# Layer-1 modulation vectors as spread half sums with their own load and sum tiles, in a two-layer hybrid trunk

## Chip, cores and metric

The kernel runs on one core of one Trainium2 chip. The metric is device microseconds of one execution, the median of three runs. Engines are named as the profile has them: TensorE (PE, with its weight load PEld), VectorE (DVE), ScalarE (ACT), GpSimd (POOL) and SyncE (SP). SP and POOL issue the DMAs here. Every engine takes its instructions in order.

## What is computed

A trunk of two layers over 1,024 tokens of width 1,024, in float32. Each layer has a mixer (attention in layer 0; retention beside an S5 state-space model in layer 1) and a convolutional feed-forward net. Both are preceded by an RMS norm that is scaled and shifted, and followed by a gate; shift, scale and gate come from the condition `c` by one large matrix per layer:

```python
cond = jax.nn.silu(c)
for i in range(DEPTH):
    mod = cond @ mod_w[i] + mod_b[i]
    sh1, sc1, g1, sh2, sc2, g2 = jnp.split(mod, 6, axis=-1)
    h = modulated_rmsnorm(x, norm1_g[i], sh1, sc1)
    ...
    x = x + g1[:, None, :] * mixed
    h = modulated_rmsnorm(x, norm2_g[i], sh2, sc2)
    x = x + g2[:, None, :] * conv_ffn(h, ffn_w_in[i], ffn_conv_w[i], ffn_conv_b[i], ffn_w_out[i])
return rmsnorm(x, final_g).astype(x.dtype)
```

`mod_w` is 2 x 1024 x 6144. The six vectors are numbered j = 0 to 5 (sh1, sc1, g1, sh2, sc2, g2), each in two halves of 512.

## The kernel before

Matrix products are made three times, with the operands split into a high and a low part (`mm3`, lines 134 to 136). Weights come by SP into a tile `stage` of 128 x 1024 (two buffers), ScalarE rounds it to the high part `wH` (line 124), VectorE subtracts to get the low part `wL` (line 125). Work that is ready is ordered by a scheduler in the tile framework: by the order of the code, with weights moved ahead by `high_priority`, and with instructions put earlier where their engine would stand idle in the scheduler's reckoning. What a reader finds in the code is therefore not the order on an engine.

The program runs in stages: start and first mixer (to about 540 us), output projection and first up phase (`up7`, PSUM tiles `c`, to about 1,080), first down phase (`down22`, tiles `acc`, to about 1,365) with the S5 constants beside it, second mixer (`mixer1`, from `mixer1_head`, to about 1,740), its output projection (`out_proj`, tiles `lin`), second up phase (to about 2,260), second down phase, final norm.

One **half sum** (`mod_sum`, lines 521 to 533) is half a vector of `cond @ mod_w`: eight loads of 128 x 512 by SP (256 KB each, line 528) into the ring `pn`, eight products on VectorE (the first at line 530, seven at line 532) into a tile of the ring `ma`, then in `mod_cols` (line 539) four matmuls with a column of ones (line 545) that add over the partitions, and a small VectorE addition of the bias (line 548). For j = 1 and 4 `mod_scale` makes the norm's scale from it. `pn` has four buffers and `ma` two, and both are general rings: the up phase's intermediate `s1`, the projections, S5 constants and the GLU's sigmoid (line 1376) take tiles of `pn` too.

Seven half sums of layer 0 are made in the first mixer, between heads. The other 13 come by `mod_all`: (layer 0, j 5, second half) at step 0 of the first down phase; layer 1's j 0 and 1 at steps 6 and 15 of it; j 2, 3 and 4 as steps M2, M3 and M4 of the retention order `RET_STEPS`; j 5 at step 2 of the second down phase. In `RET_STEPS` R0 to R3 are the heads in three parts, P projections, V values, H the load of S5 results, G the GLU (four parts). A head's last part stores its rows by POOL to DRAM (`mixd`), and the output projection loads them again (`mix`).

Of the kernel before, what the change touches and what calls it, by code (L numbers as in the profile page):

```python
# [10 lines left out]
F32 = mybir.dt.float32  # L11
# [3 lines left out]
ALU = mybir.AluOpType  # L15
# [5 lines left out]
KD = D // 128  # L21
# [8 lines left out]
S5_STEPS = 'S0 S1 X S2 P0 V0 S3 P0 V1'  # L30
RET_STEPS = 'R0 V2 P1 R0 R1 R0 R1 P1 V3 R2 R1 M2 H G R2 M3 R2 G R3 M4 G R3 R3 G'
EPS = 1e-6
# [63 lines left out]
class Trunk:  # L96
# [437 lines left out]

    def mod_all(self, l, j, ps, tag, halves=(0, 1), **kw):
        for half in halves:
            self.mod_cols(l, j, half, self.mod_sum(l, j, half), ps, tag, **kw)

# [550 lines left out]
    def mixer1(self):  # L1089
        nc, i = self.nc, self.i  # L1090
        w = i["od_w_in"][0]
        with self.pool("qkv", bufs=1) as qp, self.pool("m1ps", bufs=2, space=PSUM) as ps:
# [26 lines left out]
            def step(what):  # L1119
                kind, n = what[0], int(what[1:] or 0)  # L1120
                if kind in "RPG":
                    if what not in todo:
                        todo[what] = self.retain(n, pairs, V, rp, ps) if kind == "R" else \
                            self.project1(w, n, pairs, rp if n else qp, ps) if kind == "P" else self.glu(ps)
                    next(todo[what], None)
                else:
                    {"V": lambda: v(n), "S": lambda: s5(n), "X": gate3, "H": load_y, "M": lambda: self.mod_all(1, n, ps, "ta", bufs=3)}[kind]()

            with self.pool("wx1", bufs=2) as wx, self.pool("s5", bufs=1) as sp:
                self.wpools = [self.wp, wx]  # L1130
                for what in S5_STEPS.split():
                    step(what)
                self.wpools = [self.wp]
            with self.pool("ret", bufs=1) as rp:
                for what in RET_STEPS.split():
                    step(what)
            self.load_mix(0, 0, 4)

# [247 lines left out]
    def out_proj(self, w, l, xT, hf, x, ps, group=1, order=range(KD), between=None, fetch=False, ahead=AHEAD):  # L1386

        nc = self.nc
        hs = slice(hf * 512, hf * 512 + 512)
        for n0 in range(0, KD, group):  # L1390
            if between and n0 in TILES:
                next(between, None)
            ns = range(n0, n0 + group)
            Ws = [self.weights(w, 0, n * 128, ahead=AHEAD if n0 else ahead) for n in ns]
            if fetch:
                with self.tc.issue_after(self.loaded):
                    for n in ns:
                        nc.sync.dma_start(xT[:, n, hs], self.xs[:, n, hs])
                    if hf == 0 and n0 in (2, 4):
                        self.load_mix(1, n0 - 2, n0 + 2, 2, nc.sync)  # L1400
            for n, p in zip(ns, self.products(Ws, x, hf, ps, order=order)):
                nc.vector.scalar_tensor_tensor(xT[:, n, hs], p, self.mod[l][:, 16 + n:17 + n], xT[:, n, hs],
                                               ALU.mult, ALU.add)
# [49 lines left out]
    def up7(self, l, blocks, free, wxs, Gd):  # L1453
# [10 lines left out]
        with self.pool(f"u7ps{l}", bufs=1, space=PSUM) as ps:  # L1464
# [111 lines left out]

            Q = [{} for _ in range(NF + 2)]
            next(prep)
            for ft in range(PRE):
# [13 lines left out]
            with self.pool(f"late{l}", bufs=1) as late:  # L1593
# [6 lines left out]
                for ft in range(NF):  # L1600
                    q, n, m = Q[ft], Q[ft + 1], Q[ft + 2]
                    p6(ft, q)
                    if ft + 2 < NF:
                        head(ft + 2, m, ft + 2 < PRE)
                        if ft + 2 >= PRE:
                            p1(ft + 2, m)
                    p7(ft, q)
                    if ft + 1 < NF:
                        third(ft + 1, n)
# [72 lines left out]
    def run(self, stages=("mix0", "ffn0", "mix1", "ffn1")):  # L1682
        nc = self.nc
        with self.pool("cst", bufs=1) as self.cst, self.pool("dr", bufs=1, space=DRAM) as self.dr, \
                self.pool("wp", bufs=2) as self.wp, self.pool("tp", bufs=1) as self.tp, \
                self.pool("hp", bufs=1) as self.hp:
            self.wpools = [self.wp]
            self.s5c = self.dr.tile([4, 128, 4096], F32, name="s5c")
            with self.pool("lin", bufs=2, space=PSUM) as self.lin:
                self.mixer0(self.begin())  # L1690
            G0 = self.first_ffn_up()
            with self.pool("ub", bufs=1) as ub:
                with self.pool("s5p", bufs=1) as self.s5p, self.pool("xp", bufs=1) as xp, \
# [4 lines left out]
                    def apart(what):  # L1698
# [5 lines left out]
                        return hook  # L1704
                    hooks = {0: [lambda ps, tag: self.mod_all(0, 5, ps, tag, (1,))], 26: [apart(self.s5_small)]}
                    for j in range(2):
                        hooks[6 + 9 * j] = [lambda ps, tag, j=j: self.mod_all(1, j, ps, tag)]
                    for b in range(4):
# [7 lines left out]
                    self.mixer1_head(xT, ub, ps)  # L1716
                    self.wpools = [self.wp]
                self.mixer1()
            self.last_layer()

    def ffn_up(self, l, project):

        with contextlib.ExitStack() as es:
# [6 lines left out]
            with self.pool(f"opps{l}", bufs=4, space=PSUM) as ps:  # L1730
                w4 = X0.rearrange("p a b n -> p (a b n)").rearrange("p (a n) -> p a n", n=1024)
                self.wpools = [self.wp, Slots(wH=[w4[:, 0], w4[:, 1]], wL=[w4[:, 2], w4[:, 3]])]
                xT = project(xp, ps)
                self.wpools = [self.wp]
                self.store_x(xT, 1)
# [11 lines left out]
    def last_layer(self):  # L1747
# [10 lines left out]
        with self.pool("xp3", bufs=1) as xp, self.pool("fin", bufs=1) as fin, self.pool("wb", bufs=2) as wb, \  # L1758
# [5 lines left out]
            with self.pool("dnps", bufs=2, space=PSUM) as ps:  # L1764
                self.down22(1, xT, Gd, wb, wc, ps, lambda ps, tag: self.finish(xT, 0, ps, tag),
                            {2: [lambda ps, tag: self.mod_all(1, 5, ps, tag)]}, (self.wp, wb, wc))
            with self.pool("finps", bufs=4, space=PSUM) as ps:
# [39 lines left out]
```

## Time and profile before

| | |
|---|---|
| median of three runs | 2550.88 us (2543.54 to 2551.49) |
| profiled execution, its own time | 2545.7 us |
| its span | 2544.0 us |
| busy: PE, PEld, DVE, ACT, POOL | 95%, 78%, 72%, 45%, 7% |
| DMA | 391.56 MB, mean 154 GB/s |
| loads of modulation weights after the start | 160, 256 KB each |

A busy share is a mean over stages with different limits. PE counts as busy from the start of a matmul to its modelled end, so a full PE can still be slowed; the granted clock tells that apart. What a place costs is read from that place: how long PE stands there, at which clock, and what it waited for.

### The profile page before, as it was taken

The numbers are of one execution on the slowest core, as the hardware profiler recorded it, in microseconds if no ns is written. First come the engines' busy times: TensorE is split into PE (matmuls) and PEld (weight loads), VectorE is DVE, ScalarE is ACT, GpSimd is POOL, SyncE is SP. The second block draws the span as 40 slices with busy tenths as digits, with TensorE's granted clock in tenths as the row PEclk, the third lists the DMA queues.
The fourth block names the chain that finished last, engine by engine and source line by source line (L and its number), as shares of the span: only waits on it lengthen the run. The fifth ranks groups of instructions, "written<-read, shape, count | busy, mean of one in ns | idle before, by whom it ended". The sixth has DMA issues, their size and how long they took to land.

```text
span 2544.0 us, 32732 instructions
## 1 busy us (share of the span) xinstructions
PE 2421.3 (95%) x11599; PEld 1992.1 (78%) x11599; DVE 1839.5 (72%) x3383; ACT 1144.1 (45%) x1764; POOL 190.7 (7%) x356
## 2 busy tenths in 40 slices
PE   6999999999899999989989999979989999989997
PEld 5788888888688888877777777867868888878886
DVE  6777776666887877868996545575798787775554
ACT  4556566674544444334443344323454443424442
POOL 1000000032000000000000211201000000000000
PEclk7999999999999999999999999879999999999999
DMA  8455444466132222388774542567422222258562
GB/s 303 127 143 145 141 137 144 141 227 223 60 103 80 86 84 80 126 294 279 230 235 143 169 133 94 183 198 252 146 75 88 79 87 84 79 184 279 182 224 91
DMA packets 323524, 391.56 MB, mean 154 GB/s; under 512 B 28641, under 2 KB 203350, under 8 KB 322848
## 3 DMA queue, kind: packets, MB, share of 16 engines
q1 hardware_dynamic: 294848, 293.45, 37.3%
q0 software_dynamic: 28512, 96.02, 10.5%
q8 instruction: 91, 1.49, 0.2%
q14 instruction: 73, 0.60, 0.1%
HBM read 292.73 MB, written 70.30 MB: 143 GB/s over the span
## 4 chain that ended last, share of the span: by engine, by line
PE 71%; DVE 11%; DMA 8%; ACT 4%; issue 4%; SPq 1%; POOL 0%; DVEq 0%; ACTq 0%; POOLq 0%
PE c L136 10%; PE c L135 10%; PE c L134 10%; PE acc L135 6%; PE acc L136 6%; PE lin L134 5%; PE lin L135 5%; PE acc L134 5%; PE lin L136 5%; DMA pn<-in_mod_w_dram 2%; DVE wL L125 2%; DMA mix<-mixd 1%; DVE ma L532 1%; PE ta L738 1%; PE S L715 1%
## 5 line engine op out<-in xcount | busy, mean ns | idle before, releaser
L124 ACT ACTIVATE wH<-stage 128x1024 fp32r<-128x1024 f32 x372 | 393.0, 1059 | 538.0 <-PE acc L136 154.9
L125 DVE TENSOR_TENSOR wL<-stage,wH 128x1024 fp32r<-128x1024 f32 x372 | 452.9, 1220 | 207.3 <-ACT wH L124 200.8
L135 PE MATMUL acc<-wL,wH 128*128 128x512 f32 x704 | 280.2, 398 | 11.7 <-DVE wL L125 11.6
L136 PE MATMUL acc<-wH,wL 128*128 128x512 f32 x704 | 278.7, 396 | 0.0
L134 PE MATMUL acc<-wH 128*128 128x512 f32 x704 | 275.5, 397 | 3.2 <-DVE t2k L1568 2.4
L134 PE MATMUL lin<-h,wH 128*128 128x512 f32 x576 | 233.5, 405 | 6.2 <-ACT h L422 5.4
L135 PE MATMUL lin<-h,wH 128*128 128x512 f32 x576 | 233.7, 406 | 0.0
L136 PE MATMUL lin<-h,wL 128*128 128x512 f32 x576 | 230.3, 400 | 0.0
L134 PE MATMUL c<-h,wH 128*128 128x512 f32 x528 | 208.4, 395 | 9.2 <-ACT t2k L1589 6.5
L135 PE MATMUL c<-X,wH 128*128 128x512 f32 x528 | 207.2, 392 | 5.9 <-DVE X L1439 5.9
L134 PE MATMUL c<-X,wH 128*128 128x512 f32 x528 | 207.4, 393 | 2.6 <-ACT X L1438 2.4
L136 PE MATMUL c<-h,wL 128*128 128x512 f32 x528 | 207.0, 392 | 0.9 <-DVE wL L125 0.9
L136 PE MATMUL c<-X,wL 128*128 128x512 f32 x528 | 206.6, 392 | 0.0
L135 PE MATMUL c<-h,wH 128*128 128x512 f32 x528 | 206.4, 391 | 0.0
L135 PEld LDWEIGHTS acc<-wL,wH 128*128 128x128 f32 x704 | 134.9, 192 | 43.3 <-DVE wL L125 15.7
L134 PEld LDWEIGHTS acc<-wH 128*128 128x128 f32 x704 | 134.3, 191 | 32.5 <-DVE t2k L1568 3.2
L136 PEld LDWEIGHTS acc<-wH,wL 128*128 128x128 f32 x704 | 134.6, 191 | 28.1
L134 PEld LDWEIGHTS lin<-h,wH 128*128 128x128 f32 x576 | 110.2, 191 | 27.1 <-ACT h L422 5.7
L134 PEld LDWEIGHTS c<-h,wH 128*128 128x128 f32 x528 | 99.6, 189 | 35.8 <-ACT t2k L1589 7.3
L135 PEld LDWEIGHTS lin<-h,wH 128*128 128x128 f32 x576 | 110.2, 191 | 20.6 <-DVE h L425 1.4
L136 PEld LDWEIGHTS lin<-h,wL 128*128 128x128 f32 x576 | 110.2, 191 | 20.1 <-issue 0.2
L135 PEld LDWEIGHTS c<-X,wH 128*128 128x128 f32 x528 | 99.8, 189 | 27.5 <-DVE X L1439 6.7
(498 smaller groups left out, 5020.1 us busy)
## 6 DMA issues: line engine op xcount, KB each, us to landing
stage<-in_ffn_w_in_dram SPq DMA_DIRECT2D x92, 512.0 KB, 4.0
stage<-in_ffn_w_out_dram SPq DMA_DIRECT2D x176, 256.0 KB, 3.7
stage<-Gd SPq DMA_DIRECT2D x176, 256.0 KB, 4.0
pn<-in_mod_w_dram SPq DMA_DIRECT2D x160, 256.0 KB, 3.3
Gd<-ca POOLq DMA_DIRECT2D x88, 256.0 KB, 2.6
mix<-mixd POOLq DMA_DIRECT2D x52, 256.0 KB, 5.8
stage<-in_ev_w_in_dram SPq DMA_DIRECT2D x24, 512.0 KB, 4.0
xT<-xs SPq DMA_DIRECT2D x48, 256.0 KB, 5.1
```

The source lines that it names most:

```text
L124: nc.scalar.activation(wh[:, :n], st[:, :n], AF.Copy)
L125: nc.vector.tensor_tensor(wl[:, :n], st[:, :n], f(wh[:, :n]), ALU.subtract)
L134: nc.tensor.matmul(ps, wh, xh, start=s, stop=False)
L135: nc.tensor.matmul(ps, wh, xl, start=False, stop=False)
L136: nc.tensor.matmul(ps, wl, xh, start=False, stop=e)
L532: nc.vector.scalar_tensor_tensor(acc, st, self.cond[:, t:t + 1], acc, ALU.mult, ALU.add)
L715: nc.tensor.matmul(dst, q, KH[:, kk], start=True, stop=False)
L738: nc.tensor.transpose(pt[:, kk, j * 128:j * 128 + 128], W[j][:, (a + kk) * 128:(a + kk) * 128 + 128], self.ident)
```

## The change

The 13 late half sums are made by a generator, `mod_slow`: each step issues the next load and one product, and the ones-matmuls of a finished half sum follow at the third step of the next one. `mod_on` advances it by so many steps. The loads have tiles of their own (`ms`, two buffers), the sums too (`md`, two), in a new pool `dp`; its 8 KB per partition come from the space of POOL's software descriptors, halved to 8192 bytes. Calls stand in each tile of both up phases, at steps 2 to 25 of the first down phase, after each step of the second mixer, and six in each group of the output projection's first half. `mod_all` and the steps M2, M3 and M4 are gone.

```diff
-RET_STEPS = 'R0 V2 P1 R0 R1 R0 R1 P1 V3 R2 R1 M2 H G R2 M3 R2 G R3 M4 G R3 R3 G'
+RET_STEPS = 'R0 V2 P1 R0 R1 R0 R1 P1 V3 R2 R1 H G R2 R2 G R3 G R3 R3 G'
...
-    def mod_all(self, l, j, ps, tag, halves=(0, 1), **kw):
-        for half in halves:
-            self.mod_cols(l, j, half, self.mod_sum(l, j, half), ps, tag, **kw)
+    def mod_slow(self, todo):
...
+        def load(l, j, half, t):
+            st = self.dp.tile([128, 512], F32, tag="ms", name="ms", bufs=2)
+            c0 = j * 1024 + half * 512
+            nc.sync.dma_start(st, self.i["mod_w"][l, t * 128:t * 128 + 128, c0:c0 + 512])
+            return st
+        steps = [(*c, t) for c in todo for t in range(KD)]
+        left, st = [], load(*steps[0])
+        where = yield
+        for n, (l, j, half, t) in enumerate(steps):
+            x, st = st, load(*steps[n + 1]) if n + 1 < len(steps) else None
+            if t == 0:
+                acc = self.dp.tile([128, 512], F32, tag="md", name="md", bufs=2)
+                nc.vector.tensor_scalar(acc, x, self.cond[:, 0:1], None, ALU.mult)
+            else:
+                nc.vector.scalar_tensor_tensor(acc, x, self.cond[:, t:t + 1], acc, ALU.mult, ALU.add)
+            if t == KD - 1:
+                left.append((l, j, half, acc))
+            elif t == 2 and left:
+                c = left.pop()
+                self.mod_cols(*c, *where[:2], **where[2])
+            where = yield
+        yield
+        c = left.pop()
+        self.mod_cols(*c, *where[:2], **where[2])
...
                 for what in S5_STEPS.split():
                     step(what)
+                    self.mod_on(1, ps, "ta", bufs=3)
...
                 for what in RET_STEPS.split():
                     step(what)
+                    self.mod_on(1, ps, "ta", bufs=3)
...
+            if l and not hf:
+                self.mod_on(6, ps, "lin")
             for n, p in zip(ns, self.products(Ws, x, hf, ps, order=order)):
...
+            slow = lambda: self.mod_on(1, Banks(bank), "x")
...
                     p7(ft, q)
+                    slow()
...
+            self.mod_begin([(0, 5, 1)] + [(1, j, half) for j in range(2) for half in range(2)])
             G0 = self.first_ffn_up()
...
-                    hooks = {0: [lambda ps, tag: self.mod_all(0, 5, ps, tag, (1,))], 26: [apart(self.s5_small)]}
-                    for j in range(2):
-                        hooks[6 + 9 * j] = [lambda ps, tag, j=j: self.mod_all(1, j, ps, tag)]
+                    hooks = {s: [lambda ps, tag: self.mod_on(1, ps, tag)] for s in range(2, 26)}
+                    hooks[26] = [apart(self.s5_small)]
...
+                self.mod_begin([(1, j, half) for j in (2, 3, 4) for half in range(2)])
                 self.mixer1()
...
+                if l:
+                    self.mod_begin([(1, 5, half) for half in range(2)])
...
-                            {2: [lambda ps, tag: self.mod_all(1, 5, ps, tag)]}, (self.wp, wb, wc))
+                            {}, (self.wp, wb, wc))
...
-    nc = bacc.Bacc("TRN2", target_bir_lowering=False, num_devices=1)
+    nc = bacc.Bacc("TRN2", target_bir_lowering=False, num_devices=1, dynamic_dma_scratch_size=8192)
```

Three places show how instructions move. On SP in the first mixer, where the copies of the second head's keys (KH, KL) go out, before:

```order
L183 DMA KH<-pn 64x512
L183 DMA KL<-pn 64x512
L183 DMA KH<-pn 64x512 x4
L183 DMA KL<-pn 64x512 x4
L110 DMA stage<-in_ev_w_in_dram 128x8x128
L528 DMA pn<-in_mod_w_dram 128x512 x8
```

and in the change:

```order
L183 DMA KH<-pn 64x512
L183 DMA KL<-pn 64x512
L542 DMA ms<-in_mod_w_dram 128x512 x4
L183 DMA KH<-pn 64x512 x2
L183 DMA KL<-pn 64x512 x2
L183 DMA KH<-pn 64x512
L183 DMA KL<-pn 64x512
L183 DMA KH<-pn 64x512
L183 DMA KL<-pn 64x512
L110 DMA stage<-in_ev_w_in_dram 128x8x128
L542 DMA ms<-in_mod_w_dram 128x512 x5
L528 DMA pn<-in_mod_w_dram 128x512 x4
```

Nine loads of late half sums (`ms`) now stand between the key copies and ahead of the loads of layer 0's own sums (`pn`).

On VectorE in the second mixer, the last retention head (R3): `o` is its output, `rs` the Newton steps of its norm. Before:

```order
L1259 TENSOR_TENSOR o<-ta,T 128x256
L1259 TENSOR_TENSOR o<-ta,T 128x512
L1261 TENSOR_TENSOR o<-o,av 128x256
L1261 TENSOR_TENSOR o<-o,av 128x512
L1265 TENSOR_TENSOR o<-o,g 128x1024
L562 TENSOR_SCALAR rs<-ta 128x8
L218 TENSOR_SCALAR rs<-rs 128x8
```

and in the change:

```order
L1298 TENSOR_TENSOR o<-ta,T 128x256
L553 SCALAR_TENSOR_TENSOR md<-ms,small,md 128x512
L1300 TENSOR_TENSOR o<-o,av 128x256
L553 SCALAR_TENSOR_TENSOR md<-ms,small,md 128x512
L1298 TENSOR_TENSOR o<-ta,T 128x512
L1300 TENSOR_TENSOR o<-o,av 128x512
L553 SCALAR_TENSOR_TENSOR md<-ms,small,md 128x512
L1304 TENSOR_TENSOR o<-o,g 128x1024
L599 TENSOR_SCALAR rs<-ta 128x8
L553 SCALAR_TENSOR_TENSOR md<-ms,small,md 128x512
L218 TENSOR_SCALAR rs<-rs 128x8
```

Products of a half sum (`md`) stand between the steps of the head.

On SP in the second mixer's output projection, where weights (`stage`), residual (`xT`) and mixed rows (`mix`) are loaded. Before:

```order
L110 DMA stage<-in_od_w_out_dram 128x8x128 x2
L183 DMA mix<-mixd_12856 128x512 x4
L1398 DMA xT<-xs 128x512 x2
L1460 DMA stage<-in_ffn_w_in_dram 128x8x128
L110 DMA stage<-in_od_w_out_dram 128x8x128 x2
L1398 DMA xT<-xs 128x512 x2
```

and in the change:

```order
L110 DMA stage<-in_od_w_out_dram 128x8x128 x2
L542 DMA ms<-in_mod_w_dram 128x512
L1437 DMA xT<-xs 128x512 x2
L183 DMA mix<-mixd_12859 128x512 x4
L542 DMA ms<-in_mod_w_dram 128x512
L110 DMA stage<-in_od_w_out_dram 128x8x128 x2
L542 DMA ms<-in_mod_w_dram 128x512 x2
L1437 DMA xT<-xs 128x512 x2
```

Loads of late half sums stand ahead of the weights' loads.

## Rows read from the trace of the kernel before

**Rows 1.** The page: busy us, share, count; granted clock in 40 slices
```profile
PE 2421.3 (95%) x11599; PEld 1992.1 (78%) x11599; DVE 1839.5 (72%) x3383; ACT 1144.1 (45%) x1764; POOL 190.7 (7%) x356
...
PEclk7999999999999999999999999879999999999999
```

**Rows 2.** The page: the chain that ended last, shares by engine, then by line
```profile
PE 71%; DVE 11%; DMA 8%; ACT 4%; issue 4%; SPq 1%; POOL 0%; DVEq 0%; ACTq 0%; POOLq 0%
PE c L136 10%; PE c L135 10%; PE c L134 10%; PE acc L135 6%; PE acc L136 6%; PE lin L134 5%; PE lin L135 5%; PE acc L134 5%; PE lin L136 5%; DMA pn<-in_mod_w_dram 2%; DVE wL L125 2%; DMA mix<-mixd 1%; DVE ma L532 1%; PE ta L738 1%; PE S L715 1%
```

**Rows 3.** Groups by line: busy us, mean ns | idle before, what ended it
```profile
L532 DVE SCALAR_TENSOR_TENSOR ma<-pn,small,ma 128x512 f32<-128x512 f32 x140 | 104.3, 745 | 16.5 <-DMA pn<-in_mod_w_dram 15.2
L134 PE MATMUL lin<-mix,wH 128*128 128x512 f32 x224 | 91.9, 410 | 9.3 <-ACT pn L1376 8.7 <-DMA mix<-mixd 0.5
L545 PE MATMUL ta<-small,ma 128*128 128x1 f32 x64 | 12.2, 311 | 11.6 <-DVE ma L532 7.1 <-DVE ma L339 4.0 <-DVE rs L224 0.5
L530 DVE TENSOR_SCALAR ma<-pn,small 128x512 f32<-128x512 f32 x20 | 9.6, 480 | 0.5 <-DMA pn<-in_mod_w_dram 0.5
L545 PE MATMUL x<-small,ma 128*128 128x1 f32 x56 | 7.8, 260 | 10.0 <-DVE ma L532 9.9
```

**Rows 4.** Waits of ScalarE: total us, times, longest
```profile
ACT pn L1376 <- DVE ma L532: 14.7, 5, 12.9
```

**Rows 5.** Stretches: us, busy PE PEld DVE ACT POOL, granted clock, DMA share, GB/s
```profile
1080.00:1105.00 25.00, 17.30 (x63) 13.16 (x62) 20.80 (x32) 7.58 (x8) 1.62 (x3) 0.80 0.84 280
1645.00:1725.00 80.00, 62.94 (x309) 52.41 (x307) 58.67 (x108) 18.88 (x30) 4.84 (x9) 0.83 0.60 195
2265.00:2295.00 30.00, 22.78 (x86) 18.13 (x85) 21.40 (x34) 8.94 (x10) 2.16 (x4) 0.77 0.81 275
```

**Rows 6.** Stretches, same columns, where the change puts products
```profile
100.00:136.00 36.00, 35.89 (x198) 30.34 (x197) 32.62 (x88) 24.50 (x50) 1.10 (x2) 1.00 0.47 142
136.00:164.00 28.00, 26.96 (x160) 23.02 (x159) 14.60 (x49) 14.04 (x31) 1.62 (x3) 1.00 0.56 149
880.00:915.00 35.00, 35.00 (x156) 28.74 (x155) 29.29 (x45) 14.91 (x21) 2.16 (x4) 1.00 0.23 76
1030.00:1062.00 32.00, 32.00 (x142) 26.08 (x141) 25.43 (x40) 12.29 (x19) 1.62 (x3) 1.00 0.21 74
...
1160.00:1350.00 190.00, 177.79 (x815) 143.77 (x814) 173.20 (x381) 85.10 (x98) 5.39 (x10) 0.98 0.74 244
1350.00:1375.00 25.00, 23.07 (x101) 18.46 (x100) 14.48 (x17) 9.63 (x11) 2.16 (x4) 1.00 0.57 174
1570.00:1600.00 30.00, 27.93 (x162) 23.89 (x160) 17.04 (x38) 12.51 (x21) 2.14 (x4) 0.94 0.26 81
...
1725.00:1740.00 15.00, 15.00 (x83) 12.40 (x82) 10.70 (x28) 5.40 (x10) 4.54 (x9) 1.00 0.38 125
1740.00:1785.00 45.00, 44.03 (x190) 35.22 (x190) 19.48 (x23) 12.08 (x15) 5.12 (x10) 1.00 0.96 318
```

**Rows 7.** Chain by time, 1640 to 1730 us: start, us, what
```profile
1649.45 5.79 DMA pn<-in_mod_w_dram
...
1682.59 4.87 DMA pn<-in_mod_w_dram
```

**Rows 8.** DMA issues: engine, count, KB each, median us to landing
```profile
pn<-in_mod_w_dram SPq DMA_DIRECT2D x160, 256.0 KB, 3.3
```

**Rows 9.** Chain by time, 130 to 160 us
```profile
135.15 1.21 DVE P L726
...
139.52 3.78 DMA KH<-pn
```

**Rows 10.** Waits of VectorE, 880 to 1060 us: total us, times, longest
```profile
DVE u L1562 <- PE c L136: 30.1, 9, 3.3
```

**Rows 11.** Chain by time, 1738 to 1752 us
```profile
1739.18 6.46 DMA mixd<-t2k
...
1746.18 5.22 DMA mix<-mixd
```

More of the change, by code (lines that the diff above doesn't have):

```diff
@@ L533, in mod_sum, with mod_on, mod_begin @@
         return acc
-    def mod_all(self, l, j, ps, tag, halves=(0, 1), **kw):
-        for half in halves:
-            self.mod_cols(l, j, half, self.mod_sum(l, j, half), ps, tag, **kw)
+    def mod_slow(self, todo):
+        nc = self.nc
+        def load(l, j, half, t):
[22 more added lines that the diff above has]
+        self.mod_cols(*c, *where[:2], **where[2])
+    def mod_on(self, n, ps, tag, **kw):
+        for _ in range(n):
+            try:
+                self.slow.send((ps, tag, kw))
+            except StopIteration:
+                pass
+    def mod_begin(self, todo):
+        self.slow = self.mod_slow(todo)
+        next(self.slow)
     def mod_cols(self, l, j, half, acc, ps, tag, b=None, **kw):
@@ L1126, in step @@
                 else:
-                    {"V": lambda: v(n), "S": lambda: s5(n), "X": gate3, "H": load_y, "M": lambda: self.mod_all(1, n, ps, "ta", bufs=3)}[kind]()
+                    {"V": lambda: v(n), "S": lambda: s5(n), "X": gate3, "H": load_y}[kind]()
             with self.pool("wx1", bufs=2) as wx, self.pool("s5", bufs=1) as sp:
@@ L1684, in run @@
         with self.pool("cst", bufs=1) as self.cst, self.pool("dr", bufs=1, space=DRAM) as self.dr, \
-                self.pool("wp", bufs=2) as self.wp, self.pool("tp", bufs=1) as self.tp, \
+                self.pool("dp", bufs=1) as self.dp, self.pool("wp", bufs=2) as self.wp, self.pool("tp", bufs=1) as self.tp, \
                 self.pool("hp", bufs=1) as self.hp:
```

## Prediction

> **What bounds the kernel now.** I read the page's busy shares and granted clock first. TensorE is busy 95% of the span, and its clock is full in nearly all slices; the dip to 8 and 7 tenths in slices 27 and 28, some 1,650 to 1,780 us in, stands out [rows 1]. The chain that ended last is 71% TensorE, but 2% of it is the load of modulation weights and 1% the products on VectorE [rows 2]. So time can only be won where TensorE stands still or is slowed. The view by lines shows what ended idle time: VectorE's products waited 15.2 us for their loads, the ones-matmuls in "x" and "ta" 9.9 and 7.1 us for products, and the GLU's matmuls 8.7 us for ScalarE's sigmoid [rows 3], which itself waited 14.7 us for products [rows 4]. The sigmoid needs no modulation: it takes a slot of the four-deep ring pn, which the loads hold.
>
> **What the three places cost.** The view by stretches brackets the places where modulation is summed now [rows 5]. TensorE idles 25 - 17.30 = 7.70 us at the start of the first down phase, 80 - 62.94 = 17.06 in the retention steps and 30 - 22.78 = 7.22 at the start of the last down phase: 32.0 us. After the longer idle times its clock stands at the lower level, 1.2 instead of 2.4 GHz, for a while: the granted clock is 0.80, 0.83 and 0.77 of full speed, which is short by 0.20 x 25 + 0.17 x 80 + 0.23 x 30 = 25.5 us of full-speed work. Idle is 24% of these 135 us, so I take 24% of the 25.5 off as counted twice: 19.5. Together 51.5 us. Not all of it is modulation's. A nearby retention stretch without any modulation idles 30 - 27.93 = 2.07 of 30 us [rows 6], 7%; on 80 us that is 5.5. **The change can win about 46 us** if the waits go and nothing takes their place. That the waits are the loads' is plain in the chain by time: single loads of 5.79 and 4.87 us stand on it there [rows 7].
>
> **What the change moves.** The work stays: 13 half sums of 8 products, 104 loads of 256 KB, 13 x 0.48 + 91 x 0.75 = 74 us of VectorE [rows 3], 13 groups of ones-matmuls. Nothing is computed less. The loads leave pn for a ring of two tiles of their own, the sums get a ring of two. In the new order, placing each product by its neighbours and their times in the old trace, 16 products stand in the first mixer (72 to 176 us), 16 in the first up phase (880 to 913 and 1033 to 1060), 8 at 1091 to 1152, 8 among the S5 constants to 1265, 8 at 1352 to 1364, 8 at 1573 to 1588, 8 at 1648 to 1677, 8 at 1724 to 1738, 8 at 1743 to 1772, and 16 at 1780 to 1831. The last down phase has none left. So the title's spreading holds only in part: the scheduler pulled sums ahead of the code that asks for them and bunched several.
>
> A bunch has a price. With two tiles, the third load starts only when the first product is done, and a load takes 3.3 us to land in the median [rows 8], 5.8 where the transfers are crowded [rows 7]. Adjacent products then go one per (3.3 + 0.75) / 2 = 2.0 us or slower, and VectorE, in order, holds whatever stands behind; SP, in order too, holds the weight loads behind a load that has no tile. The Trainium skill ("DMA: Bandwidth & Descriptors", the fit of fixed cost and bandwidth) has 2.0 us plus bytes over 436e3, an estimate of 2.6 us for 256 KB; by it the pace would be 1.7 us and the prices below a fifth lower. The trace's longer times count, since other transfers run beside.
>
> The prices, in us of TensorE time, low to high, and what I take:
> (1) First mixer: 16 products are 12 us; VectorE is free for 3.4 and 13.4 us in its two stretches [rows 6]. The eighth product's load stands on SP behind K copies, the last of which leave near 139.5 us [rows 9], so it lands near 143.5, while VectorE comes to it after the bias step that ends at 136.4 [rows 9]: some 6 us in which softmax work is held. The scheduler put projection matmuls there as filler. 0 to 8, I take 3.
> (2) First up phase: 12 us for VectorE, which in those stretches has 5.7 and 6.6 us free [rows 6] and waits 30.1 us in nine times for TensorE [rows 10]. TensorE is ahead of nothing here that VectorE must give within 3 us. 0 to 3, I take 0; were VectorE's wait for TensorE gone, 3 us.
> (3) S5 constants: VectorE is busy 173.20 of 190 us [rows 6], but about as many products leave this part as come. -2 to 4, I take 0.
> (4) Start of the second mixer: 6 us of products and about 5 of waits within 15 us, ahead of the weight splits TensorE starts on; it idles 1.93 us there already [rows 6]. 0 to 6, I take 2.
> (5) Second query projection, 1573 to 1588: three adjacent products wait some 4 us, ahead of the rotation that TensorE's transposes need. 0 to 8, I take 3.
> (6) Retention, 1648 to 1677: the third product of the half sum waits for a load that starts with the first one's end, about 5 us, as now [rows 7]; GLU results behind it keep PSUM. 0 to 8, I take 4.
> (7) Last retention head, 1724 to 1738: six of eight products now stand between its output, its Newton steps and its store. VectorE is busy 10.70 of 15 us [rows 6], so 6 us of products and as much waiting do not fit into 4.3. Behind it come the store and load of the mixed rows, 6.46 and 5.22 us on the chain [rows 11]: what is late here is late for the output projection. 0 to 14, I take 6.
> (8) Output projection, near 1775: the last scale half sum's loads stand on SP between weight and residual loads, where the DMA engines are busy 0.96 [rows 6]; four ones-matmuls wait for it ahead of TensorE's weights work. 0 to 12, I take 5.
> (9) The 16 products to 1831 have VectorE half free. 0 to 4, I take 0.
> The smaller descriptor space for POOL's queue I cost at nothing, 0 to 3: POOL is busy 7% and its order hardly changes. In the up phases the four ones-matmuls use the accumulators' ring of three, whose slots are refilled a whole tile later: nothing.
>
> **Sum.** 46 - (3 + 0 + 0 + 2 + 3 + 4 + 6 + 5 + 0) = 23 us won. Against the profiled execution, 2545.7 us, that gives 2522.7. The median of the three runs is 5.2 us above it; I carry half of that, 2.6: **2525 us**, 25.9 or 1.0% below the median of before. All lows give 51.5 + 2 = 53.5 won, 2495; all highs cost 70, 24 lost, 2572.
>
> **Rivals.** *Full gain:* two tiles are enough, since half of the loads come early and wait for their products; the bunches cost 5 us or less. Then 41 or more is won, 2500 to 2507. For it: the waits of VectorE for TensorE [rows 10]. Against it: the single loads on the chain with four tiles, not two [rows 7]. *Nothing moves:* the waits come back at (5) to (8), with the clock falling after each as in [rows 5]; 23 us become 46: 2548. For it: the same in-order queues. *Slower:* one mechanism, the output projection starved by SP. Between 1740 and 1785 the engines move 318 GB/s at a share of 0.96 [rows 6]; the order adds 8 loads, 2.1 MB or 6.6 us, into these 45 us and sets each ahead of a weight load, which it holds until VectorE has freed a tile: four places here. Four further places follow to 1800. If five of the eight hold SP for a load's 5.8 us, weights come 29 us later; the two weight tiles in hand serve 48 matmuls, 11 us at 190 in 45 us [rows 6], so TensorE would stand 18 us and lose 25.5 / 32 of that again by the clock, 32 together. With (7) at its high end and the other terms as taken the balance is 46 - 12 - 14 - 32 = -12: 2560; with (1) and (6) high as well 2569. It decides from the point where a held weight load outlasts the weights in hand. The Trainium skill speaks for it ("DMA: Bandwidth & Descriptors", queues, rings and completion order): an engine takes turns between the queues that have work, so SP's added loads slow POOL's loads of the mixed rows as well; the share of 0.96 agrees that there is no room. *The change doesn't do what it says* is part of this: sums bunched ahead are what the order shows, not a spread.
>
> **How the numbers follow.** The measurement tells about 0.3%, 7.7 us, from no change: below 2543.2 is faster, above 2558.6 slower. Forecast, 2507 to 2543: 0.64. Full gain, below 2507: 0.14. Nothing moves, 2543 to 2558.6: 0.13. Slower: 0.09. Faster is 0.64 + 0.14 = 0.78. The range 2500 to 2551 leaves out the best part of the full gain and the worse half of the last two cases, about 0.2.
>
> **What would show it.** Right: no ones-matmul and no GLU matmul that waits for a product or a sigmoid in the retention steps; granted clock 1.0 at the start of both down phases; the last down phase's idle under 3 us in its first 30. Each price has its sign: (1) VectorE waiting for the new tile near 140 us; (6) and (7) the same near 1650 and 1730, and a store of the mixed rows later after the last GLU; (8) ones-matmuls into "lin" waiting for the product. It would be wrong if TensorE's idle time in 1570 to 1785 stayed as large as now, or if weight splits in the output projection waited for their loads.

## The result and the profile after

The changed kernel takes **2520.8 us** in the median of four runs (2519.67 to 2522.58), the kernel before 2547.2 in the runs beside it: 26.4 us less, with a ratio of 0.9892, 95% interval 0.9873 to 0.9911. The forecast was 2525, with 2500 to 2551 as its range. The profiled execution has a span of 2518.0 us against 2544.0.

The page of the changed kernel, busy times and granted clock (its kernel.py has some 40 lines more ahead of most of the code, so L545 is now L582, L1376 is L1415):

```profile
PE 2412.1 (96%) x11599; PEld 1985.8 (79%) x11599; DVE 1836.4 (73%) x3383; ACT 1144.7 (45%) x1764; POOL 190.9 (8%) x356
...
PEclk7999999999999999999999999899999999999999
```

The work is the same, 11599 matmuls and 3383 instructions on VectorE. Counted from 1, the low digits of [rows 1] are an 8 in slice 26 and a 7 in slice 27, 1590 to 1717 us (the prediction has them one slice late); now the 8 stands and the 7 is gone. The groups of the moved sums, in the view by lines (columns as in [rows 3]):

```profile
L553 DVE SCALAR_TENSOR_TENSOR md<-ms,small,md 128x512 f32<-128x512 f32 x91 | 67.9, 746 | 35.3 <-DMA ms<-in_mod_w_dram 34.9
L551 DVE TENSOR_SCALAR md<-ms,small 128x512 f32<-128x512 f32 x13 | 6.2, 479 | 0.5 <-DMA ms<-in_mod_w_dram 0.5
```

VectorE's products wait more for their loads than before, 34.9 us where [rows 3] has 15.2 for all 140. What changed is who waits behind them. TensorE's waits in the retention steps of the changed kernel, all that the view shows:

```profile
PE ta L134 <- DVE t2k L1257: 0.4, 1, 0.4
PE ta L595 <- ACT t2k L1302: 0.4, 1, 0.4
PE ta L1190 <- ACT pn L1187: 0.3, 1, 0.3
PE lin L135 <- DMA mix<-mixd: 0.2, 1, 0.2
```

No ones-matmul and no GLU matmul is among them; the 8.7 us on the sigmoid and the 7.1 on products [rows 3] are gone. The view by stretches, here for the stretches of the changed kernel that hold about the work of [rows 5]:

```profile
1084.00:1100.00 16.00, 14.92 (x67) 12.12 (x66) 9.55 (x17) 5.84 (x7) 1.08 (x2) 0.89 0.69 233
1643.00:1692.00 49.00, 48.25 (x270) 41.44 (x268) 33.99 (x65) 18.55 (x29) 4.84 (x9) 0.99 0.39 126
2246.00:2270.00 24.00, 18.58 (x72) 14.59 (x71) 15.52 (x21) 9.06 (x11) 2.15 (x4) 0.86 0.71 248
```

The retention steps that took 80 us take 49, with 0.75 us of idle time and a clock of 0.99 where there were 17.06 and 0.83. The first down phase starts with 1.08 us idle in place of 7.70. The last one still idles 5.42 us of 24. The granted clock at the start of both is not full: 0.89 and 0.86.

**Where the time went, by stretch.** I compare when the N-th matmul starts in both traces (ones-matmuls left out, 11343 are left), and take how much the distance between the two grows from one time of the old trace to the next; minus is time won. "Predicted" is worked out from the terms on record: the idle time of a place and 0.76 of its clock loss, less 5.5 us in the retention steps, plus the prices. The second column of the change is from a later run, and up4 is an experiment below, also with two traces. The same code in two executions differs by up to 3.6 us in a stretch (retention, 31.6 and 28.0), so smaller differences say little.

```
stretch of the      what                     predicted  change      up4
old trace, us                                           1st   2nd   1st   2nd
50 to 180           first mixer, price (1)      +3.0    -0.6  +0.8  +0.6  +0.3
675 to 1075         first up phase, (2)          0.0    +2.7  +2.1 +11.2 +13.9
1075 to 1160        start of first down phase  -11.5   -11.4 -11.8  -5.6  -6.2
1160 to 1350        S5 constants, (3)            0.0    +0.5  -0.9  -8.2  -9.5
1350 to 1375        second mixer's start, (4)   +2.0    +4.0  +2.8  -0.2  -0.4
1375 to 1570        S5 steps                     0.0    +0.1  -0.1  -0.2  -0.1
1570 to 1645        second queries, (5)         +3.0    +1.5  +1.1  -1.9  -2.2
1645 to 1725        retention, (6) in it       -17.9   -31.6 -28.0 -33.2 -30.2
1725 to 1853        (7), (8) and (9)           +11.0   +12.7 +13.6  +1.0  +1.1
1853 to 2250        last up phase                0.0    +1.4  +1.3  +2.3  +2.0
2250 to 2300        start of last down phase   -12.5    -6.7  -6.6  -6.1  -7.1
all else                                         0.0    +1.9  +3.0  +6.3  +2.5
whole                                          -22.9   -25.6 -22.9 -34.0 -36.3
```

### The profile page after: what moved, and what is told of

Same layout as the page of the kernel before. It is cut to its first block, busy times and chain, and to the rows that moved or that the text cites. A ratio compares the mean times of both kernels' runs of the same rounds, so it can differ in the third digit from the quotient of the medians.

```text
span 2518.0 us, 32681 instructions
## 1 busy us (share of the span) xinstructions
PE 2412.1 (96%) x11599; PEld 1985.8 (79%) x11599; DVE 1836.4 (73%) x3383; ACT 1144.7 (45%) x1764; POOL 190.9 (8%) x356
## 4 chain that ended last, share of the span: by engine, by line
PE 72%; DVE 10%; DMA 8%; issue 4%; ACT 4%; SPq 1%; POOL 1%; DVEq 0%; ACTq 0%; POOLq 0%
PE c L134 11%; PE c L136 11%; PE c L135 10%; PE lin L135 5%; PE lin L134 5%; PE acc L135 5%; PE lin L136 5%; PE acc L136 5%; PE acc L134 5%; DMA ms<-in_mod_w_dram 2%; DVE wL L125 2%; PE ta L775 1%; DMA mix<-mixd 1%; PE S L752 1%; PE S L753 1%
## 5 line engine op out<-in xcount | busy, mean ns | idle before, releaser
L134 PEld LDWEIGHTS lin<-h,wH 128*128 128x128 f32 x576 | 109.9, 191 | 28.6 <-ACT h L422 6.9
L136 PEld LDWEIGHTS c<-h,wL 128*128 128x128 f32 x528 | 100.3, 190 | 26.2 <-DVE wL L125 2.3
```

The lines of the kernel that those rows point to most:

```text
L134: nc.tensor.matmul(ps, wh, xh, start=s, stop=False)
L136: nc.tensor.matmul(ps, wl, xh, start=False, stop=e)
```

## The experiments

**What the sums still cost: one product each.** Each late half sum keeps its first load and product and leaves out the other seven. Edit, in the new generator:

```diff
+            if t:
+                return None
             st = self.dp.tile([128, 512], F32, tag="ms", name="ms", bufs=2)
...
-            else:
-                nc.vector.scalar_tensor_tensor(acc, x, self.cond[:, t:t + 1], acc, ALU.mult, ALU.add)
             if t == KD - 1:
```

> Leaves out seven of the eight products and loads of each of the 13 late half sums (the first product alone goes into the ones-matmuls), so 91 loads and 91 products are gone and the rest stands as in the changed kernel. Aligned by matmul count, the changed kernel gives back 4.0 us between 1350 and 1375 us and 12.8 us between 1725 and 1853 us (times of the kernel before). Theory: these are the sums' own prices, (4), (7) and (8); they go away and little else changes: 2504 us, 2500 to 2508. Rival: the output projection is held by its own weights and by the mixed rows, which TensorE now reaches sooner, and the sums only stand beside them: 2514 to 2520 us, with the 12.8 us still there.

Measured: 2499.5 us, ratio 0.9799 (0.9782 to 0.9816), 21 us under the change and far from the rival's time. By stretch its gains against the kernel before are -7.2 us at the S5 constants, -0.9 at the second mixer's start, -28.6 in the retention steps, and +6.4 past 1725 us. So the sums still cost 6 to 8, 4 to 5, 0 and 6 to 7 us in these places. Theory and rival each get half of the last one: half of the 12.7 us goes with the seven products. What is left there belongs either to the ones-matmuls, first loads and first products, which still stand, or to the projection itself; up4, with no sums there at all, has +1.0, so it is the former.

**The tiles alone.** The kernel before, with its calls where they were; its late half sums take both new rings (`mod_late` is `mod_sum` with these two tiles), and the descriptor space is the smaller one:

```diff
+    def mod_late(self, l, j, half):
+        nc, i = self.nc, self.i
+        acc = self.dp.tile([128, 512], F32, tag="md", name="md", bufs=2)
...
+            st = self.dp.tile([128, 512], F32, tag="ms", name="ms", bufs=2)
...
-            self.mod_cols(l, j, half, self.mod_sum(l, j, half), ps, tag, **kw)
+            self.mod_cols(l, j, half, self.mod_late(l, j, half), ps, tag, **kw)
```

> The kernel before with its late half sums asked for where they were, but with loads and sums in the new rings of two (and the smaller descriptor space). The scheduler still pulls two half sums into the first mixer and those of the last down phase forward into 1680 to 1752 us. Theory: the place decides, five half sums crowd the retention steps, and what the tiles alone bring is the sigmoid's slot in the old ring (8.7 us of TensorE's idle time, some 12 with the clock) and the emptied last down phase (6.6 us): 2535 us, 2528 to 2545. Rival: the shared ring was the whole trouble and the places don't matter: 2524 us or less.

Measured: 2545.1 us, ratio 0.9989 (0.9979 to 0.9999): some 3 us where the theory had 13. The rival, that the shared ring was the whole trouble, is out: the place decides. The trace, of an execution 6 us slower than the median, shows where the gain stays: -8.0 us at the start of the first down phase, -21.7 in the retention steps and -6.9 at the last down phase, but +8.8 at the S5 constants and +24.9 in the stretch from 1725 to 1853. Six half sums stand in 1656 to 1802 us of this kernel, and TensorE's longest waits there, and the stretch itself, are

```profile
PE ta L558 <- DVE md L545: 6.7, 2, 6.1
PE ta L587 <- DVE rs L224: 5.2, 1, 5.2
```

```profile
1705.00:1800.00 95.00, 78.32 (x345) 64.85 (x344) 49.31 (x82) 21.41 (x29) 9.69 (x18) 0.86 0.73 236
```

The waits for the ones-matmuls and for a Newton step (L224) that VectorE holds behind products have moved 50 us later: 16.68 us idle and a clock of 0.86. This is the rival "nothing moves", made by leaving half of the change out.

**The places alone.** The changed kernel with its loads in the old ring, each asked for with its product:

```diff
-            st = self.dp.tile([128, 512], F32, tag="ms", name="ms", bufs=2)
+            st = self.tmp(tag="pn")
...
-            x, st = st, load(*steps[n + 1]) if n + 1 < len(steps) else None
+            x = load(l, j, half, t)
```

> The changed kernel, but its loads go back into the old ring of four and each is asked for with its product, not one call ahead; the sums keep their own tiles. In the order no product stands in the first mixer any more; the half sums begin at 687 us and four are summed in the first up phase. Theory: the ring matters only where other users of it wait, in the retention steps, so that the GLU waits come back there and the down phases stay free: 2532 us, 2525 to 2542. Rival: only the places matter: 2516 to 2523 us. Second rival: in the up phases too the loads hold slots that ScalarE's steps need: 2545 us or more.

Measured: 2545.7 us, ratio 0.9986 (0.9970 to 1.0001), the time of the second rival. The theory has the places backwards. The retention steps win all the same, -31.8 us, with loads in the old ring, so there the loads' ring does not matter; the up phases lose, 13.3 us in the first and 13.6 in the last, where only two half sums are summed, and the second queries lose 8.3. TensorE there does not stop for long; it is late by a little in every tile. VectorE's waits in 690 to 1070 us of this kernel:

```profile
DVE u L1603 <- PE c L136: 41.8, 15, 3.0
...
DVE md L553 <- DMA pn<-in_mod_w_dram: 11.7, 14, 3.6
...
DVE md L551 <- DMA pn<-in_mod_w_dram: 1.4, 2, 0.7
```

and the same stretch of the changed kernel:

```profile
DVE u L1603 <- PE c L136: 48.7, 15, 3.3
...
DVE md L553 <- DMA ms<-in_mod_w_dram: 2.0, 3, 1.0
```

TensorE's weight loads then wait for VectorE's splits, in this kernel and in the changed one:

```profile
PEld c L136 <- DVE wL L125: 8.6, 14, 0.8
```

```profile
PEld c L136 <- DVE wL L125: 0.3, 1, 0.3
```

So the other half of the edit pays in the up phases and not in the retention steps. Which part of it, the ring or the load one call ahead, was not tried apart. The second rival's mechanism does not show: in the view of this stretch ScalarE waits for no product and no load of modulation weights. SyncE's view and timeline speak for the load that is asked for too late:

```profile
SPq L1501 <- DVE wL L125: 316.2, 38, 11.7
...
SPq L542 <- DMA pn<-in_mod_w_dram: 3.7, 2, 2.5
SPq L542 <- DVE md L553: 1.8, 2, 1.0
```

```profile
744.29 18.23 SPq L1501 DMA_DIRECT2D stage<-in_ffn_w_in_dram  x3
762.57 0.57 SPq L542 DMA_DIRECT2D pn<-in_mod_w_dram  x1
```

The loads of modulation weights (L542) waited for a tile only four times, 5.5 us; they leave right behind weight loads (L1501) that wait for VectorE. The one of 762.57 us is the load for which the product of 767.31 us waits.

**The price past 1,725 us, by moving the products earlier.** Three calls after each S5 step, and what is left of the six in the output projection:

```diff
                 for what in S5_STEPS.split():
                     step(what)
-                    self.mod_on(1, ps, "ta", bufs=3)
+                    self.mod_on(3, ps, "ta", bufs=3)
...
-                self.mod_on(6, ps, "lin")
+                self.mod_on(2, ps, "lin")
```

> The changed kernel with three products after each S5 step of the second mixer instead of one, so that fewer of them are left for the output projection; in the order eight products stand past 1,700 us instead of some 32. Theory: the prices (7) and (8), 12.8 us by the alignment, are paid for products in 1725 to 1810 us; two thirds or more of them go: 2510 us, 2506 to 2515. Rival: the bunches cost in the S5 steps what they cost later, since two tiles serve one product in 2 us wherever they stand: 2518 to 2526 us.

Measured: 2531.9 us, ratio 0.9931 (0.9908 to 0.9954), by the median 11 us behind the change and slower than the rival too. The price at the output projection did go, +1.1 us in place of +12.7; but the S5 steps now lose 13.6, as the rival has it. Three half sums stand between 1492 and 1574 us, and TensorE's stretch in it is

```profile
1545.00:1572.00 27.00, 20.77 (x95) 17.32 (x94) 14.95 (x27) 5.13 (x9) 1.06 (x2) 0.68 0.57 189
```

6.23 us idle, and the clock at 0.68. A bunch that costs some 13 us in one place costs as much in the next. The trace is of the fastest of the four executions, 2522.6 us; what the other three lose beyond it, 7 to 14 us, it does not show.

**Four tiles instead of two.**

```diff
-            st = self.dp.tile([128, 512], F32, tag="ms", name="ms", bufs=2)
+            st = self.dp.tile([128, 512], F32, tag="ms", name="ms", bufs=4)
...
-    nc = bacc.Bacc("TRN2", target_bir_lowering=False, num_devices=1, dynamic_dma_scratch_size=8192)
+    nc = bacc.Bacc("TRN2", target_bir_lowering=False, num_devices=1, dynamic_dma_scratch_size=4096)
```

> The changed kernel with four tiles for the loads instead of two (the descriptor space halved once more to make room). VectorE's products wait 34.9 us for loads in the changed kernel. Theory: the price of a bunch is that the third load starts only when the first product is done; with four tiles the pace doubles and half of the 19 us that are left goes: 2511 us, 2505 to 2516. Rival: where the waits lie the DMA engines are 0.93 busy and a load takes 5 to 7 us whatever the ring, and SP issues more of them ahead of the weights: 2518 to 2526 us.

Measured: 2518.7 us, ratio 0.9881 (0.9854 to 0.9909), no different from the change (the trace is of its slowest execution, 2525.4 us). The waits fall as the theory has it, and the time doesn't follow:

```profile
DVE md L553 <- DMA ms<-in_mod_w_dram: 9.3, 10, 4.4
...
DVE md L551 <- DMA ms<-in_mod_w_dram: 6.5, 2, 4.7
```

That is 15.8 us in place of 35.4. The products of the second queries' half sum start in 1570 to 1578 us instead of 1570 to 1586, so two tiles do set the pace of a bunch. But a load's median from issue to landing rises from 3.5 to 4.3 us, and the stretch 1570 to 1645 loses 5.3 us where it lost 1.5: where the time that the products no longer wait was lost is not settled by this run.

**The smaller descriptor space alone**, on the kernel before:

```diff
-    nc = bacc.Bacc("TRN2", target_bir_lowering=False, num_devices=1)
+    nc = bacc.Bacc("TRN2", target_bir_lowering=False, num_devices=1, dynamic_dma_scratch_size=8192)
```

> The kernel before with the smaller descriptor space for POOL's queue alone. The same instructions in the same order. Theory: costs nothing, ratio 0.998 to 1.002, 2547 us. Rival: POOL's stores of GLU rows wait for free descriptors, 2550 us or more.

Measured: 2548.3 us, ratio 1.0001 (0.9986 to 1.0016): nothing, as costed. Its trace also says how far stretches of the same instructions differ between executions: some 3 us (-3.0 at the S5 constants, +3.0 in the S5 steps).

**All early, in the up phase.** The first eleven half sums begin with the first up phase, four products a feature tile; the calls in the second mixer and the output projection go:

```diff
-            slow = lambda: self.mod_on(1, Banks(bank), "x")
+            slow = lambda: self.mod_on(1 if l else 4, Banks(bank), "x")
...
-            self.mod_begin([(0, 5, 1)] + [(1, j, half) for j in range(2) for half in range(2)])
+            self.mod_begin([(0, 5, 1)] + [(1, j, half) for j in range(5) for half in range(2)])
```

The run up3 has 3 in place of 4, up5 has 5.

> The first eleven half sums asked for in the first up phase, four products after each of its feature tiles; none in the first down phase, the second mixer or the output projection. The order has nearly all of them before 1,075 us. With one product each, the run one_product is 21 us under the changed kernel; aligned by matmul count its advantage lies at the S5 constants (7.8 us), the start of the second mixer (4.9) and the retention's end with the output projection (6.5). Theory: VectorE has 33 of 200 us free there, 3.1 us a feature tile, one product a tile is paid already and three more take 2.2, so the phase carries them and all three prices go: 2504 us, 2499 to 2510. Rival: two tiles serve one product in about 2 us, so four in a row hold VectorE 5 us or more a tile, the GLU steps behind them come late and TensorE waits in each of 22 tiles, 1 us or more each: 2520 to 2545 us.

> As up4, with three products a feature tile and the last 24 in the first down phase, one a hook as in the changed kernel. Theory: the up phase carries three, the S5 constants keep their price of 7.8 us and the start of the second mixer too, the price past 1,700 us goes: 2514 us, 2508 to 2518. Rival, as for up4 but smaller: 2520 to 2532 us.

> As up4, with five products a feature tile, so that the first eleven half sums end before the first down phase begins. In up4 the last half sums reach into the first down phase, whose start gains 3.0 us there against 8.8 in the changed kernel; each half sum costs TensorE 1.0 us in the up phase, its four ones-matmuls. Theory: the start of the down phase comes free and VectorE still carries five a tile (3.75 us, less than the 4.3 it has with none): 2503 us, 2498 to 2508. Rival: five fill VectorE, GLU steps come late in some tiles: 2509 to 2525 us.

Measured: up4 2509.0 us, ratio 0.9837 (0.9810 to 0.9865); up3 2518.6, 0.9880 (0.9851 to 0.9909); up5 2511.3, 0.9849 (0.9823 to 0.9875). The theory holds in its direction, and by size it was 5 to 8 us too hopeful; up5's time lies in its rival's range. In up4 the three prices go (table above), and the up phase takes 11.2 to 13.9 us for it. Most of that is named in the view by lines of up4:

```profile
L582 PE MATMUL c<-small,md 128*128 128x1 f32 x96 | 11.4, 239 | 0.0
```

These are the ones-matmuls of twelve half sums, eight instructions each, with no idle time before them: 11.4 / 12 = 0.95 us a half sum, ten of the twelve in the first up phase. TensorE is the bound there, so they are paid in full. The row for 675 to 1075 us of up4,

```profile
675.00:1075.00 400.00, 394.98 (x1751) 321.04 (x1750) 361.12 (x553) 164.19 (x231) 20.51 (x38) 1.00 0.41 127
```

has VectorE busy 361.12 of 400 us, 90%, and its products wait 6.6 + 1.1 us for loads there; TensorE idles 5.02 us, against 1.92 in the same stretch of the kernel before. So VectorE carries the products, and the rival's waits of TensorE, 1 us or more in each of 22 tiles, do not show. In up3's trace 32 products stand past the up phase, and the S5 constants lose 6.5 us for it, so it is no better than the change. up5 wins the start of the down phase back (-11.2) and pays 14.9 us in the up phase: no different from up4.

**All early, from the first mixer on.** The later calls go as in up4.

```diff
                     self.mod_cols(0, j, h, acc, self.lin, "lin")
+                self.mod_on(6, self.lin, "lin")
...
-            slow = lambda: self.mod_on(1, Banks(bank), "x")
+            slow = lambda: self.mod_on(1 if l else 2, Banks(bank), "x")
...
+            self.mod_begin([(0, 5, 1)] + [(1, j, half) for j in range(5) for half in range(2)])
             with self.pool("lin", bufs=2, space=PSUM) as self.lin:
```

> The first eleven half sums asked for from the first mixer on, six products after each of its eight units, the rest two a feature tile in the first up phase; none later but the last two half sums. Theory: TensorE has short idle times in the mixer's attention in which the ones-matmuls and products hide, and the up phase keeps fewer: 2502 us, 2497 to 2509. Rival: a burst of six products at one in 2 us holds softmax steps on VectorE in each unit, 2 us or more each: 2512 to 2530 us.

Measured: 2513.1 us, ratio 0.9862 (0.9837 to 0.9887), between the change and up4, and in the rival's range: the mixer's eight units lose 13.4 us (50 to 675), and the up phase still 6.3. But the loss is not one of 2 us in each unit, as the rival has it: some 7 us lie between 520 and 540 us and 4 between 160 and 180. What stops TensorE there was not followed.

**The change and up4 once more, side by side.**

> The changed kernel once more, beside up4 on the same chip. 2520 us, 2516 to 2524, ratio 0.987 to 0.991.

> up4 once more, beside the changed kernel. Theory: it stays ahead of the change: 2509 us, 2504 to 2513, some 11 us under it. Rival: the chip or the day made the difference: within 5 us of the changed kernel.

Measured: the change 2523.3 us, ratio 0.9896 (0.9878 to 0.9914); up4 2511.1, 0.9850 (0.9828 to 0.9873). up4 beats both kernels, the change by some 12 us, 0.5%; the intervals of the two ratios do not touch.

## Why the prediction was right, and where it was not

The forecast won 23 us against its profiled execution; the two traces of the change win 25.6 and 22.9. The prediction was right in its direction, its size and the main of its mechanism: the waits at the three places go, and bunches take part of it back. That the sum came out so close is luck in part: the retention steps won 10 to 14 us more than forecast, the last down phase 6 less, and the other rows of the table together came some 5 us dearer. Two of the signs of being right failed: the clock at the starts of the down phases is 0.89 and 0.86 in the profiled execution, not 1.0, and the last one idles 5.42 us. Of the signs of being wrong, TensorE's idle time fell from 22.20 us in 1570 to 1785 to 7.43 in the same work (1567 to 1759 us); the other came, and is told under (7) to (9). In detail:

- **What can be won, 46 us.** Taken place by place, it was wrong by as much as 13 us and right in the sum. *First down phase:* 11.5 predicted, 11.4 and 11.8 measured.
- *Retention:* 21.9 predicted before price (6); up4, with no sums there, wins 33.2 and 30.2. The term was mis-sized by two deductions, the 5.5 us "not modulation's" and the 24% taken off the clock loss. Without them it is 17.06 + 0.17 x 80 = 30.7. The nearby stretch without modulation that gave the 5.5 [rows 6] was a poor stand-in: freed, these steps idle 0.75 us in 49. Whether the 24% is to be taken off is less sure: in the first down phase the sum is 11.5 with it and 12.7 without, and the measured 11.4 and 11.8 are within the noise of both.
- *Last down phase:* 12.5 predicted, 6.7 and 6.6 measured, and the sign "idle under 3 us" failed: it is 5.42. I had not named what is late next. The chain by time of the changed kernel shows it:

```profile
2252.14 4.90 issue
2257.06 5.61 DMA Gd<-ca
2262.82 1.06 ACT wH L124
2263.91 1.24 DVE wL L125
```

  The view names the store of the GLU's last rows, 5.61 us, ahead of ScalarE's next rounding, and TensorE waits 4.95 us in one piece. The rounding itself reads `stage`, half of which is loaded back from the stored rows, and no such load is on the chain; so it is the store, or a load close behind it. All kernels that leave no sums in this phase win about the same there, 6.1 to 7.1 us, own_tiles among them. No run took the store away, and the cause stays open that far.
- **(1) First mixer, 3 taken:** nothing, -0.6 and +0.8, within what equal instructions differ by. VectorE did wait for the new tile there, 2.3 us in three pieces.
- **(2) Up phases, 0 taken:** +2.7 and +2.1 in the first, +1.4 and +1.3 in the last. I had costed the ring that the ones-matmuls use, and not the ones-matmuls: 0.95 us a half sum, four half sums.
- **(3) S5 constants, 0 taken:** +0.5 and -0.9, right as a balance. It hid a chance: with most of the products gone from there up4 wins 8.2 and 9.5, and one_product, with one in eight, 7.2.
- **(4) and (5), 2 and 3 taken:** +4.0 and +2.8, and +1.5 and +1.1; within their bounds.
- **(6), 4 taken:** the change wins 31.6 and 28.0 in the retention steps against up4's 33.2 and 30.2, so about 2, no more than two executions differ by.
- **(7), (8) and (9), 11 taken:** +12.7 and +13.6. The sum is right; of the signs only one is. TensorE's waits in 1695 to 1840 us of the changed kernel:

```profile
PE c L134 <- ACT pn L1534: 3.8, 2, 3.1
PE lin L611 <- DVE rs L224: 2.8, 1, 2.8
PE lin L134 <- DVE xT L1443: 1.9, 1, 1.9
...
PE lin L135 <- DMA mix<-mixd: 0.5, 1, 0.5
```

  The mixed rows, which (7) had late, cost 0.5 us, and no ones-matmul into "lin" is in the list, which (8) had as its sign (only the weight load of one waited, 0.4 us). In the projection TensorE waits for VectorE's own results, a residual update (L1443, it frees the accumulator) and a norm's Newton steps (L224), and at the start of the up phase for a copy by ScalarE (L1534), 3.8 us where the kernel before has 1.4. VectorE's timeline shows the update of 1735 us behind a product that waited for its load (start, us, what, in brackets the idle time before it):

```profile
1721.32 1.23 DVE L125 TENSOR_TENSOR wL<-stage,wH 128x1024 fp32r<-128x1024 f32 x1 [9.24 <-ACT wH L124]
...
1734.58 0.75 DVE L553 SCALAR_TENSOR_TENSOR md<-ms,small,md 128x512 f32<-128x512 f32 x1 [3.53 <-DMA ms<-in_mod_w_dram]
1735.25 1.40 DVE L1443 SCALAR_TENSOR_TENSOR xT<-lin,mod,xT 128x512 f32<-128x512 f32 x2
```

  The weights come late too, as (8) and the rival "slower" had it, and as the second sign of being wrong said; but they did so before. ScalarE's waits for them in 1715 to 1800 us of the kernel before, and in 1690 to 1785 us of the changed one:

```profile
ACT wH L124 <- DMA stage<-in_od_w_out_dram: 17.2, 4, 10.3
ACT X L124 <- DMA stage<-in_od_w_out_dram: 13.8, 4, 6.0
```

```profile
ACT X L124 <- DMA stage<-in_od_w_out_dram: 14.1, 3, 8.0
...
ACT wH L124 <- DMA stage<-in_od_w_out_dram: 13.9, 2, 11.5
```

  They sum to 31.0 us before and 28.0 after, so the sign tells nothing, and that loads of modulation weights starve the projection is not shown. In the chain by time of the changed kernel a load of modulation weights is followed by one of the projection's weights:

```profile
1723.01 5.46 DMA ms<-in_mod_w_dram
1728.53 7.45 DMA stage<-in_od_w_out_dram
```

  and the stretch around it, in the view by stretches, has no room on the DMA engines, a share of 1.04 at 348 GB/s (0.95 at 317 in 1750 to 1775 us of the kernel before):

```profile
1717.00:1742.00 25.00, 21.56 (x89) 16.45 (x88) 13.00 (x18) 7.37 (x9) 2.17 (x4) 0.93 1.04 348
```

  TensorE stood 25 - 21.56 = 3.44 us there and not that rival's 18; so (7) to (9) cost 13 us in all and not its 14 + 32 = 46.
- **The pace of a bunch.** I took 2.0 us a product with two tiles; the half sum at 1570 to 1586 us has seven steps in 16 us, 2.3. The Trainium skill ("DMA: Bandwidth & Descriptors", the fit in "Anatomy of one DMA — SWDGE (gpsimd) path") gives an estimate of 2.6 us for 256 KB; the fit is for transfers that GpSimd issues, and these are SyncE's. The trace agrees with it for the shortest of the 104 loads alone (2.6 us; median 3.5, longest 7.1), so it does not give the pace.

## What to carry to other kernels

Work that needs nothing from its surroundings should be put where the engine that it needs has time and nobody stands behind it; moving it is worth the idle time it caused, and each new place is priced by what is queued behind it there. A ring of its own with the load asked for ahead is half of the matter: the ring without the places won next to nothing (0.9989), and the places without both won nothing either (0.9986). When a stall is taken out, take nothing off its idle time and clock loss by a stretch that only looks alike, and then name what is late next: it cut the gain of the last down phase to half.

## What had not been expected of the hardware

Four matmuls by a single column, whose TensorE time I had left out, take eight instructions and 0.95 us of TensorE in the up phase, where TensorE is the bound: more than one of the eight products takes VectorE (0.746 us). And doubling the tiles for the loads cut VectorE's waits from 35.4 to 15.8 us with no gain clear of the noise, while the median load went from 3.5 to 4.3 us.
